# The pooling stage of a two-layer decoder trunk: scale by a broadcast transfer, whole-row loads of x, another order of the work, and the norms' epsilon on VectorE

## The chip, the core and the metric

The kernel runs on one core of a Trainium2 chip. A core has five engines that run side by side and wait for one another by semaphores: TensorE (PE, matmuls into the accumulators in PSUM), VectorE (DVE, elementwise work and statistics), ScalarE (ACT, casts and activations), GpSimd (POOL) and SyncE (SP, which issues transfers). Each engine takes its instructions strictly in the order of the program. The metric is device time in microseconds (us) of one execution; the kernel before takes 951.83 us, the median of three runs (950.6 to 952.05).

## The reference

The input is `x`, 512 tokens of 1024 float32. Layer 0 mixes tokens by pooling, layer 1 by attention; each is followed by a gated feed-forward, and each of the four steps ends in a layer norm. The part that matters here is layer 0's mixer and the norms:

```python
ALPHA = (2.0 * DEPTH) ** 0.25          # DEPTH = 2
POOL_WINDOWS = (2, 4, 8, 16)           # one group of 256 columns each

def _layernorm(x, g, b):
    mu = jnp.mean(x, axis=-1, keepdims=True)
    var = jnp.mean(jnp.square(x - mu), axis=-1, keepdims=True)
    return (x - mu) * lax.rsqrt(var + LN_EPS) * g + b

def _multiscale_pool(x, w, scale):
    ...                                # per group: mean over the last `win` tokens
    mixed = jnp.einsum('bsgc,gcd->bsgd', pooled - xg, w)
    return mixed.reshape(B, S, D) * scale

for i in range(DEPTH):
    h = pool(x) if i == 0 else diff_attention(x)
    x = _layernorm(ALPHA * x + h, ...)
    x = _layernorm(ALPHA * x + _swiglu(x, w_gate[i], w_up[i], w_down[i]), ...)
```

## The kernel before

**Numbers in two parts.** Float32 products are made from float32r operands: each operand is split into a high part (a cast on ACT) and a low part (the difference, on DVE or POOL), and `mm3` adds three products. So every block of data and of weights costs one cast, one subtraction and three matmuls for one.

**The order** is written out by hand: `tc.manual_schedule()` keeps each engine's instructions in the order of the Python code, and semaphores are put in for the data. The weights come in pieces of 128 x 1024 (512 KB), `raw0`, `raw1`, ..., through five buffers that SP fills in turn (`fetch`); `ready(c)` splits them up to number c.

**The pooling stage.** The 512 tokens are four blocks of 128 (s = 0 to 3). Pooling over tokens is a matmul with banded matrices, built on the core: `fh` (with its low part `fl`, which is not zero for the first 16 tokens only) for block 0, `bh` for the others. The helpers, in the order of their first use:

- `load_x(s)` loads block s of x into `res`; `split_x(s, d)` splits one half of its columns. In blocks 2 and 3 the low parts are made on POOL.
- `WARM` matmuls on zeros (`still`) stand first on PE.
- `spread(c)` makes 512 columns of the scale over all 128 partitions, by a matmul of one row of ones with one row of scale (`scrow`), into the accumulators `sc0` and `sc1`; `scale_weights(c)` multiplies the pool weights `raw0` and `raw1` by them on DVE, and `pool_weights(c)` splits them.
- `low(t, ks)` pools into tokens 0 to 255 from block t (t = 0, 1), `high(blocks, ks)` into tokens 256 to 511 from blocks 1 to 3. `split_pooled(half, groups)` brings the sums from PSUM to SBUF in two parts.
- `mixed(s, d)` multiplies block s by half d of the pool weights (12 matmuls of 256 columns), `summed(s, d)` adds it to `res` (`residual`) and takes the statistics (`stat`).
- `spread_of(n, s)` makes of them mean and variance (`mv`) and the factor `rs`: epsilon is added on POOL, and the power −0.5 taken on POOL. `norm(n, s)` applies them to `res` on DVE.
- `transposed(n, s)` turns a normed block on PE in eight matmuls into accumulators `pt`; `turned_half` applies gain and bias (ACT, one half of block 1 on DVE as `second`), `split_turned` splits into `xt`, the operand of the feed-forward.

`ready`, `tbh`, `tbl`, `ohr` and `lines_sum` in between split the first feed-forward weights and prepare the table of attention's biases.

**What follows.** `ffn(0)`, `attention`, `ffn(1)`. A feed-forward starts with three (layer 0) or two (layer 1) plain column blocks, tokens 0 to 255 first; blocks 2 and 3 of the layer are transposed between those products (`late`). Then come column blocks by Strassen products (`strassen(k)`, k from 2), with sums of weights (`weight_sums`, two DVE passes, then stores) and of hidden rows (`sum_hidden`) on DVE beside them. The last feed-forward ends with four norms in two passes each, which also add gain and bias (`norm` with `done`), and with the stores. Attention's end (`gather`) loads the table of activation functions for the next feed-forward (`preload_act_table_set`).

## Time and profile before

| | us |
|---|---|
| median of three runs | 951.83 (950.6 to 952.05) |
| the profiled execution | 952.55 |
| its span, first to last instruction | 950.8 |
| TensorE busy | 935.4 (98% of the span) |
| VectorE busy | 819.2 (86%) |
| ScalarE busy | 503.8 (53%) |
| POOL busy | 119.7 (13%) |
| HBM traffic | 206 GB/s over the span |

The profile is one execution, and every row below has its times in us from the start of the span. A timeline row has start, duration, engine, line, operation, what it writes and reads (the program's names, without buffer numbers) and, in brackets, how long the engine stood idle before it and what released it. PE is TensorE's matmuls. A busy PE is not PE at its peak: the rows also show how far apart the matmuls start.

### The profile page before, as it was taken

Reading aid. Unit: us, or ns where it says so; the run is one execution under the profiler, and the core shown is the slowest. Engines: PE = TensorE matmul, PEld = TensorE weight load, DVE = VectorE, ACT = ScalarE, POOL = GpSimd, SP = SyncE. Lnnn points to the kernel's source line nnn. Section 1 sums busy time; section 2 is a strip of 40 time slices with the busy share of each in tenths; the row PEclk is TensorE's granted clock in tenths of the full one; section 3 lists DMA queues with packets and bytes.
Section 4 is the critical chain, followed back from the end, with each engine's and each line's share of the span. In section 5 each row is a group of like instructions: output and inputs, shape, how many; then the busy total and the mean of one; then the engine's idle time right before and its main releaser. Section 6 shows DMA issues by size and latency. Waiting matters only on the chain.

```text
span 950.8 us, 16040 instructions
## 1 busy us (share of the span) xinstructions
PE 935.4 (98%) x6263; PEld 858.0 (90%) x6263; DVE 819.2 (86%) x1199; ACT 503.8 (53%) x807; POOL 119.7 (13%) x157
## 2 busy tenths in 40 slices
PE   9999999999999999999999999999999999999995
PEld 8899999999988888988888888999999999988884
DVE  6999999999988798688777676799999999987797
ACT  5563455555563467665566553834545544654450
POOL 5122111110001201000000000311111110002102
PEclk9999999999999999999999999999999999999998
DMA  7189998886877965423222122389988885878962
GB/s 255 44 250 270 298 293 264 261 241 221 260 241 261 361 206 166 145 89 100 77 80 80 65 90 89 115 254 283 285 248 257 263 274 203 250 237 287 321 212 88
DMA packets 73933, 196.88 MB, mean 207 GB/s; under 512 B 6595, under 2 KB 18019, under 8 KB 73858
## 3 DMA queue, kind: packets, MB, share of 16 engines
q1 hardware_dynamic: 34272, 113.92, 36.1%
q0 software_dynamic: 15952, 47.31, 18.8%
q10 hardware_dynamic: 23634, 34.64, 10.0%
q8 instruction: 49, 0.80, 0.3%
q14 instruction: 26, 0.21, 0.1%
HBM read 159.12 MB, written 36.72 MB: 206 GB/s over the span
## 4 chain that ended last, share of the span: by engine, by line
PE 85%; DVE 8%; ACT 3%; issue 2%; POOL 1%; POOLq 0%; DVEq 0%; ACTq 0%
PE A L851 21%; PE P L917 13%; PE C L851 10%; PE Q L917 6%; PE B L851 5%; PE s L1134 2%; PE v L125 2%; PE v L126 2%; PE v L127 2%; PE q L126 2%; PE q L127 1%; PE q L125 1%; PE k L125 1%; PE k L127 1%; PE k L126 1%
## 5 line engine op out<-in xcount | busy, mean ns | idle before, releaser
L605 DVE TENSOR_TENSOR raw<-raw,raw 128x1024 f32<-128x1024 f32 x72 | 87.8, 1219 | 0.6
L107 ACT CAST xs<-hid 128x512 fp32r<-128x512 f32 (+1 forms) x60 | 34.7, 581 | 28.4 <-DVE hid L770 28.4
L108 DVE TENSOR_TENSOR xs<-hid,xs 128x512 fp32r<-128x512 f32 (+1 forms) x60 | 38.4, 641 | 7.8 <-ACT xs L107 7.8
L227 ACT ACTIVATE y<-pt,gbT 128x128 f32<-128x128 f32 x92 | 34.6, 457 | 18.5 <-PE pt L208 18.4
L1144 ACT ACTIVATE p<-p,mn 128x128 f32<-128x128 f32 (+3 forms) x64 | 35.4, 554 | 14.9 <-DVE mn L1139 14.9
L701 POOL DMA_DIRECT2D b<-in_wall x24 | 18.1, 798 | 152.3 <-DMA tsum<-b 73.0
L762 POOL DMA_DIRECT2D xs<-ssum x24 | 17.4, 727 | 141.9 <-PE Q L917 119.3
L108 POOL TENSOR_TENSOR sql<-sq,sqh 128x512 fp32r<-128x512 f32 x7 | 9.1, 1295 | 165.3 <-ACT sqh L107 165.3
L877 ACT ACTIVATE sg<-sg 128x512 f32<-128x512 f32 x18 | 11.4, 633 | 33.2 <-DVE sg L870 33.2
L1139 DVE CUSTOM_DVE_ANT_0 p<-s,bias 128x128 f32<-128x128 f32 (+3 forms) x64 | 28.1, 485 | 0.0
L701 POOL DMA_DIRECT2D hid<-in_wall x20 | 14.8, 742 | 93.2 <-DVE g_42l L611 24.3
L171 POOL TENSOR_SCALAR rs<-mv 128x1 f32<-128x1 f32 x16 | 7.8, 490 | 147.2 <-DVE mv L169 143.2
L108 DVE TENSOR_TENSOR xt<-y,xt 128x512 fp32r<-128x512 f32 x23 | 15.6, 687 | 12.5 <-ACT xt L107 12.2
L738 ACT CAST v<-u 128x512 fp32r<-128x512 f32 x22 | 13.7, 621 | 22.6 <-DVE u L736 22.6
L862 ACT COPY hid<-C 128x512 f32<-128x512 f32 x18 | 10.6, 587 | 26.0 <-PE C L851 24.1
L163 DVE BATCH_NORM_STATS2 st<-res 128x6 f32<-128x512 f32 x32 | 22.2, 695 | 1.1
L108 DVE TENSOR_TENSOR heads<-k,heads 128x512 fp32r<-128x512 f32 x8 | 5.5, 692 | 20.2 <-ACT heads L107 20.2
L866 DVE TENSOR_TENSOR hid<-C,hid 128x512 f32<-128x512 f32 x18 | 12.4, 690 | 11.6 <-PE C L851 10.0
L702 POOL DMA_DIRECT2D b<-in_wall x12 | 14.7, 1229 | 56.8 <-DMA b<-in_wall 47.2
L1158 DVE SCALAR_TENSOR_TENSOR p<-p,sm,p 128x128 f32<-128x128 f32 (+3 forms) x32 | 17.6, 551 | 1.1
L107 ACT CAST heads<-k 128x512 fp32r<-128x512 f32 x8 | 4.7, 588 | 26.2 <-PE k L127 26.2
L1134 PE MATMUL s<-heads 64*128 64x256 f32 (+2 forms) x192 | 17.9, 330 | 0.0
(1154 smaller groups left out, 3822.2 us busy)
## 6 DMA issues: line engine op xcount, KB each, us to landing
raw<-in_wall SPq DMA_DIRECT2D x122, 512.0 KB, 4.4
r<-tsum SPq DMA_DIRECT2D x40, 512.0 KB, 4.4
b<-in_wall POOLq DMA_DIRECT2D x36, 512.0 KB, 6.0
hid<-in_wall POOLq DMA_DIRECT2D x30, 512.0 KB, 6.6
r<-in_wall SPq DMA_DIRECT2D x30, 512.0 KB, 4.5
tsum<-b ACTq DMA_DIRECT2D x24, 512.0 KB, 4.8
ssum<-v ACTq DMA_DIRECT2D x22, 512.0 KB, 3.7
tsum<-hid ACTq DMA_DIRECT2D x20, 512.0 KB, 5.1
```

The source lines that it names most:

```text
L107: nc.scalar.copy(dst_h, src)
L108: (low or nc.vector).tensor_tensor(dst_l, src, dst_h.bitcast(F32), op=ALU.subtract)
L125: nc.tensor.matmul(acc, ah, bh, start=start, stop=False)
L126: nc.tensor.matmul(acc, ah, bl, start=False, stop=False)
L127: nc.tensor.matmul(acc, al, bh, start=False, stop=stop)
L227: nc.scalar.activation(y[:, k, :], src, AF.Identity, bias=b, scale=g)
L605: tt(t, raws[pair[0]], raws[pair[1]], op=ALU.add)
L701: nc.gpsimd.dma_start(out=t[:, j], in_=src[:, j])
L851: nc.tensor.matmul(o, w[:, c], x[:, kk, :], start=p in ("P1", "Q5", "P2") and f + kk + e == 0, stop=p in ("Q4", "Q3", "P2") and (f, kk, e) ...
L917: nc.tensor.matmul(accs[s], x[:, k, r], y[:, c], start=first and k == 0 and e == 0, stop=last and k == m - 1 and e == 2, skip_group_check= ...
L1134: nc.tensor.matmul(accs[c][:, :wide], a[r, qs], b[r, :wide], start=i == 0, stop=i == 2)
L1144: nc.scalar.activation(p, p, AF.Exp, bias=mn[:, q, c : c + 1], scale=-1.0, accum_out=sm[:, q, c : c + 1],)
```

## The change

- The scale comes by one transfer on SP's queue, broadcast to 128 partitions (`scale`); the row, the ones, the two matmuls of `spread` and their accumulators go. `scale_weights` reads SBUF.
- x is loaded in four transfers of whole rows instead of eight of half rows.
- There are 22 warm-up matmuls instead of 5, and `fl` is 256 columns wide (zero beyond the 16, filled by ACT), so the low-part matmuls of block 0 are too.
- The accumulators for tokens 256 to 511 are taken from the start, and the order is another: block 1's high part follows the low parts at once, blocks 2 and 3 come later and one by one, their low parts and that of weight 2 are made on DVE, and `pool_weights` works in halves.
- The norms' epsilon is added on DVE, all 16 times.
- One pair of weight sums in each feed-forward stands behind the first Strassen product instead of a plain block. The line that loads the activation table stands behind its loop.

```diff
-WARM = 5
+WARM = 22
     def load_x(s):
-        for d in range(2):
-            c = slice(d * 512, (d + 1) * 512)
-            nc.sync.dma_start(out=res[:, s, c], in_=x[s * P : (s + 1) * P, c])
+        nc.sync.dma_start(out=res[:, s, :], in_=x[s * P : (s + 1) * P, :])
...
-        nc.gpsimd.tensor_scalar(rs, mv[:, 1:2], scalar1=EPS, scalar2=None, op0=ALU.add)
+        nc.vector.tensor_scalar(rs, mv[:, 1:2], scalar1=EPS, scalar2=None, op0=ALU.add)
         nc.gpsimd.tensor_tensor(rs, rs, mhalf, op=ALU.pow)
...
         load_x(0)
-        scrow = pp.tile([1, D], F32, name="scrow")
-        nc.scalar.dma_start(out=scrow, in_=pscale)
...
         load_x(1)
         fetch(1)
+        scale = pp.tile([P, D], F32, name="scale")
+        nc.sync.dma_start(out=scale, in_=pscale.broadcast_to([P, D]))
         load_x(2)
...
-        fl = pp.tile([P, 4, 16], F32R, name="fl")
+        fl = pp.tile([P, 4, 256], F32R, name="fl")
...
-        nc.vector.memset(fl.bitcast(F32), 0.0)
+        nc.scalar.copy(
+            fl.rearrange("p g (a t) -> p (g a) t", a=2), still.unsqueeze(1).to_broadcast([P, 8, P])
+        )
...
         for i in range(WARM):
-            nc.tensor.matmul(scb[0][:, 0:P], still, still, start=True, stop=True)
+            nc.tensor.matmul(warm[:, 0:P], still, still, start=True, stop=True)
...
-                    mm(o[:, :16], xk(xnh, 0, k), fl[:, g, :], start=False, stop=False)
+                    mm(o, xk(xnh, 0, k), fl[:, g, :], start=False, stop=False)
...
-        spread(0)
         low(0, range(4))
         low(0, range(4, 8))
-        spread(1)
         low(1, range(8))
-        for g in range(4):
-            made[1, g] = bank(f"pool1_{g}")
         scale_weights(0)
-        split_x(2, 0, nc.gpsimd)
-        split_x(2, 1, nc.gpsimd)
-        high((1, 2), range(4))
-        scale_weights(1)
+        high((1,), range(8))
         pool_weights(0)
-        split_x(3, 0, nc.gpsimd)
         split_pooled(0, 0, 1)
         mixed(0, 0)
+        split_x(2, 0)
+        split_x(2, 1)
+        high((2,), range(8))
+        scale_weights(1)
+        split_pooled(0, 2, 3)
         pool_weights(1)
-        split_pooled(0, 2, 3)
-        split_x(3, 1, nc.gpsimd)
-        high((1, 2), range(4, 8))
+        mixed(1, 0)
         mixed(0, 1)
-        ready(3, nc.gpsimd)
+        split_x(3, 0)
+        split_x(3, 1)
+        summed(0, 0)
...
-        mixed(1, 0, 1)
-        summed(0, 0, 1)
+        mixed(1, 1)
+        summed(0, 1)
         spread_of(0, 0)
+        ready(3)
...
-        summed(3, 0, 1)
+        summed(3, 0)
         norm(0, 2)
+        ready(5)
+        summed(3, 1)
         spread_of(0, 3)
-        ready(5)
         norm(0, 3)
...
-                if f in (3, 5, 7):
-                    weight_sums()
...
+                    if k == SPLIT[0] and p == "P1":
+                        weight_sums()
```

Three places show what this does to the queues. The first is the start of PE's. `still` is the zero operand, `sc0` the scale's accumulator, `pool0_0` the first group of tokens 0 to 255. Before:

```order
L314 MATMUL sc0_140<-still_100 128x128 x5
L345 MATMUL sc0_140<-scrow_81,one_101 128x512
L352 MATMUL pool0_0_136<-fh_97,xt_63 128x256
L353 MATMUL pool0_0_136<-fl_98,xt_63 128x16
L354 MATMUL pool0_0_136<-fh_97,xt_63 128x256
```

Now:

```order
L312 MATMUL pool1_0_134<-still_96 128x128 x22
L351 MATMUL pool0_0_130<-fh_93,xt_63 128x256
L352 MATMUL pool0_0_130<-fl_94,xt_63 128x256
L353 MATMUL pool0_0_130<-fh_93,xt_63 128x256
L351 MATMUL pool0_0_130<-fh_93,xt_63 128x256
```

Seventeen warm-ups came in, the one-row matmul went, and the 16-column matmul has 256 columns.

The second place is DVE's queue from the scaling of the pool weights on. `raw` are the weights, `pw` their low parts, `pooled` the low parts of the pooled sums, `xt<-res` those of x, `mix` the mixer's results. Before:

```order
L326 TENSOR_TENSOR raw0_87<-raw0_87,sc0_140 128x512 x2
L326 TENSOR_TENSOR raw1_91<-raw1_91,sc1_141 128x512 x2
L108 TENSOR_TENSOR pw0l_66<-raw0_87,pw0h_65 128x1024
L108 TENSOR_TENSOR pooled_64<-pool0_0_136,pooled_64 128x2x256
L108 TENSOR_TENSOR pooled_64<-pool0_1_137,pooled_64 128x2x256
L108 TENSOR_TENSOR pw1l_250<-raw1_91,pw1h_249 128x1024
L108 TENSOR_TENSOR pooled_64<-pool0_2_138,pooled_64 128x2x256
L108 TENSOR_TENSOR pooled_64<-pool0_3_139,pooled_64 128x2x256
L156 SCALAR_TENSOR_TENSOR res_67<-res_67,mix0_0_235 128x512
```

Now:

```order
L325 TENSOR_TENSOR raw0_83<-raw0_83,scale_85 128x512 x2
L337 TENSOR_TENSOR pw0l_66<-raw0_83,pw0h_65 128x512 x2
L106 TENSOR_TENSOR pooled_64<-pool0_0_130,pooled_64 128x2x256
L106 TENSOR_TENSOR pooled_64<-pool0_1_131,pooled_64 128x2x256
L106 TENSOR_TENSOR xt_63<-res_67,xt_63 128x512 x2
L325 TENSOR_TENSOR raw1_88<-raw1_88,scale_85 128x512 x2
L106 TENSOR_TENSOR pooled_64<-pool0_2_132,pooled_64 128x2x256
L106 TENSOR_TENSOR pooled_64<-pool0_3_133,pooled_64 128x2x256
L337 TENSOR_TENSOR pw1l_277<-raw1_88,pw1h_276 128x512 x2
L106 TENSOR_TENSOR xt_63<-res_67,xt_63 128x512 x2
L154 SCALAR_TENSOR_TENSOR res_67<-res_67,mix0_0_236 128x512
L161 BN_STATS st0_0_313<-res_67 128x6
```

Four passes over x (blocks 2 and 3) came in between, and the second weight's scaling moved behind the first pooled sums.

The third place is DVE's queue at the end of the stage, around the norms of blocks 2 and 3 (`mv0_2`, `mv0_3`). Before:

```order
L156 SCALAR_TENSOR_TENSOR res_67<-res_67,mix2_0_391 128x512
L163 BN_STATS st0_2_494<-res_67 128x6
L156 SCALAR_TENSOR_TENSOR res_67<-res_67,mix2_1_392 128x512
L163 BN_STATS st0_2_494<-res_67 128x6
L169 BN_AGGR mv0_2_498<-st0_2_494 128x2
L156 SCALAR_TENSOR_TENSOR res_67<-res_67,mix3_0_461 128x512
L163 BN_STATS st0_3_504<-res_67 128x6
L156 SCALAR_TENSOR_TENSOR res_67<-res_67,mix3_1_462 128x512
L163 BN_STATS st0_3_504<-res_67 128x6
L181 TENSOR_SCALAR res_67<-res_67,mv0_2_498,rs0_2_500 128x1024
L169 BN_AGGR mv0_3_509<-st0_3_504 128x2
L108 TENSOR_TENSOR w4l_517<-raw4_289,w4h_516 128x1024
```

Now:

```order
L161 BN_STATS st0_2_505<-res_67 128x6
L154 SCALAR_TENSOR_TENSOR res_67<-res_67,mix2_1_402 128x512
L161 BN_STATS st0_2_505<-res_67 128x6
L167 BN_AGGR mv0_2_509<-st0_2_505 128x2
L169 TENSOR_SCALAR rs0_2_511<-mv0_2_509 128x1
L154 SCALAR_TENSOR_TENSOR res_67<-res_67,mix3_0_472 128x512
L161 BN_STATS st0_3_515<-res_67 128x6
L179 TENSOR_SCALAR res_67<-res_67,mv0_2_509,rs0_2_511 128x1024
L106 TENSOR_TENSOR w4l_521<-raw4_317,w4h_520 128x1024
L154 SCALAR_TENSOR_TENSOR res_67<-res_67,mix3_1_473 128x512
L161 BN_STATS st0_3_515<-res_67 128x6
L167 BN_AGGR mv0_3_526<-st0_3_515 128x2
```

The norm of block 2 moved ahead of the second residual of block 3, weight 4's low part with it, and each aggregate is followed by the epsilon.

More of the change, by code (lines that the diff above doesn't have):

```diff
@@ L299, in trunk @@
         for t in (fh[:, :, 0:144], bh[:, :, P : P + 144]):
+            nc.vector.tensor_copy(t[:, :, P:], near[:, :, P:])
             nc.vector.tensor_tensor(t[:, :, :P], near[:, :, :P], own, op=ALU.subtract)
-            nc.vector.tensor_copy(t[:, :, P:], near[:, :, P:])
         xnh, xnl = (
@@ L309, in split_x @@
             split(xnh[:, s, c], xnl[:, s, c], res[:, s, c], low=low)
-        made = {(0, g): bank(f"pool0_{g}") for g in range(4)}
-        scb = [bank(f"sc{c}") for c in range(2)]
+        made = {(i, g): bank(f"pool{i}_{g}") for i in range(2) for g in range(4)}
+        warm = made[1, 0]
         for i in range(WARM):
-            nc.tensor.matmul(scb[0][:, 0:P], still, still, start=True, stop=True)
-        split(fh[:16, :, 0:16], fl[:16], d0)
+            nc.tensor.matmul(warm[:, 0:P], still, still, start=True, stop=True)
+        split(fh[:16, :, 0:16], fl[:16, :, 0:16], d0)
         split_x(0, 0)
@@ L325, in scale_weights, with pool_weights @@
                 r = raw[:, j * 512 : (j + 1) * 512].rearrange("p (k e) -> p k e", k=2)
-                nc.vector.tensor_tensor(
-                    r,
-                    r,
-                    scb[c][:, j * GW : (j + 1) * GW].unsqueeze(1).to_broadcast([P, 2, GW]),
-                    op=ALU.mult,
+                e0 = c * 512 + j * GW
+                engine.tensor_tensor(
+                    r, r, scale[:, e0 : e0 + GW].unsqueeze(1).to_broadcast([P, 2, GW]), op=ALU.mult
                 )
-        def pool_weights(c):
+        def pool_weights(c, between=lambda: None):
             h, l = weight_pair(f"pw{c}") if c else first_pair
-            split(h, l, raws.pop(c))
+            raw = raws.pop(c)
+            cols = [slice(j * 512, (j + 1) * 512) for j in range(2)]
+            for cc in cols:
+                nc.scalar.copy(h[:, cc], raw[:, cc])
+            between()
+            for cc in cols:
+                nc.vector.tensor_tensor(l[:, cc], raw[:, cc], h[:, cc].bitcast(F32), op=ALU.subtract)
             pw.append((h, l))
@@ L342, in xk @@
             return t[:, s, k * P : (k + 1) * P]
-        def spread(c):
-            mm(scb[c], one, scrow[:, c * 512 : (c + 1) * 512], start=True, stop=True)
         def low(t, ks):
@@ L451, in trunk @@
         norm(0, 0)
+        transposed(0, 0)
+        split_pooled(1, 0, 1)
         summed(1, 1)
         spread_of(0, 1)
-        transposed(0, 0)
-        split_pooled(1, 0, 1)
-        norm(0, 1)
         mixed(2, 0)
         split_pooled(1, 2, 3)
+        norm(0, 1)
+        mixed(2, 1)
         transposed(0, 1)
-        mixed(2, 1)
         pts = [turns.pop((0, i)) for i in range(2)]
```

7 lines of the change are left out of this document (2 added, 5 removed).

## The prediction

> **What bounds the kernel now.** I read the page first: its busy times, then the shares of the chain that ended last.
>
> ```profile
> span 950.8 us, 16040 instructions
> PE 935.4 (98%) x6263; PEld 858.0 (90%) x6263; DVE 819.2 (86%) x1199; ACT 503.8 (53%) x807; POOL 119.7 (13%) x157
> PE 85%; DVE 8%; ACT 3%; issue 2%; POOL 1%; POOLq 0%; DVEq 0%; ACTq 0%
> ```
>
> TensorE (PE) carries nearly everything, so a change outside it counts only where PE waits or where PE is slow. PE's timeline of the first 19 us shows slow work: columns are start, duration, instruction, and in brackets the idle time before it.
>
> ```profile
> 1.04 2.50 PE L314 MATMUL sc<-still 128*128 128x128 f32 x10 [1.04 <-DVE still L265]
> 3.48 2.07 PE L345 MATMUL sc<-scrow,one 1*128 1x512 f32 x2
> ...
> 10.12 0.41 PE L352 MATMUL pool<-fh,xt 128*128 128x256 f32 x1
> 10.34 0.21 PE L353 MATMUL pool<-fl,xt 128*128 128x16 f32 x1
> ...
> 10.90 2.07 PE L345 MATMUL sc<-scrow,one 1*128 1x512 f32 x2
> 12.90 0.58 PE L356 MATMUL pool<-bh,xt 128*128 128x256 f32 x1
> 13.28 0.41 PE L357 MATMUL pool<-bh,xt 128*128 128x256 f32 x1
> ...
> 17.97 0.40 PE L367 MATMUL pool<-bh,xt 128*128 128x256 f32 x1
> 18.18 0.31 PE L366 MATMUL pool<-bh,xt 128*128 128x256 f32 x1
> 18.33 0.28 PE L367 MATMUL pool<-bh,xt 128*128 128x256 f32 x1
> 18.45 0.28 PE L366 MATMUL pool<-bh,xt 128*128 128x256 f32 x1
> ```
>
> The 22 starts from 13.28 to 17.97 lie 0.213 us apart; from 18.33 on they lie 0.115 apart. The page's slices print a full clock there:
>
> ```profile
> PEclk9999999999999999999999999999999999999998
> ```
>
> But the spacing says that PE ran at about half rate until 18.2 and doubled there, 5.3 us after a dense run of 128-row, 256-column matmuls began at 12.90. Ahead of it stood one-row matmuls (L345) and 16-column ones (L353), and the rate did not rise behind them.
>
> After 19 us the stage depends more and more on VectorE (DVE). Three rows of its timeline, and PE's one large wait of the stage, at the transposes of block 2:
>
> ```profile
> 26.32 0.69 DVE L163 BATCH_NORM_STATS2 st<-res 128x6 f32<-128x512 f32 x1
> 26.93 0.80 DVE L181 TENSOR_SCALAR res<-res,mv,rs 128x1024 f32<-128x1024 f32 x1
> 27.65 0.68 DVE L156 SCALAR_TENSOR_TENSOR res<-res,mix 128x512 f32<-128x512 f32 x1
> ...
> 44.94 1.06 PE L208 MATMUL pt<-ident,res 128*128 128x128 f32 x8 [1.00 <-DVE mv L169]
> ```
>
> From 44.94 to 375 PE's timeline has no bracket, so the start of these transposes is the mark of the stage: what it gains, the kernel gains. After that brackets over 0.2 come at two norms only:
>
> ```profile
> 375.40 1.09 PE L208 MATMUL pt<-ident,res 128*128 128x128 f32 x8 [0.24 <-DVE res L181]
> 592.23 1.09 PE L208 MATMUL pt<-ident,res 128*128 128x128 f32 x8 [0.77 <-DVE res L181]
> ```
>
> Last, the tail. PE's last matmul starts at 938.60, yet the kernel ends at 950.8 behind four norms:
>
> ```profile
> 930.58 0.20 DVE L169 BATCH_NORM_AGGREGATE mv<-st 128x2 f32<-128x12 f32 x1
> 930.81 1.42 DVE L188 SCALAR_TENSOR_TENSOR res<-res,mv,gb 128x512 f32<-128x512 f32 x2
> 930.87 0.78 POOL L171 TENSOR_SCALAR rs<-mv 128x1 f32<-128x1 f32 x1 [18.71 <-DVE mv L169]
> 931.74 0.92 POOL L172 TENSOR_TENSOR rs<-rs,mhalf 128x1 f32<-128x1 f32 x1
> 932.70 1.41 DVE L192 SCALAR_TENSOR_TENSOR res<-res,rs,gb 128x512 f32<-128x512 f32 x2 [0.47 <-POOL rs L172]
> ...
> 942.37 0.68 DVE L904 SCALAR_TENSOR_TENSOR res<-res,P 128x512 f32<-128x512 f32 x1
> ...
> 938.60 0.39 PE L917 MATMUL P<-d_41h,xs 128*128 128x512 f32 x1
> ```
>
> **The change, part by part.**
>
> *Warm-up and first matmuls.* Ten halves of five warm-ups took at most 3.48 − 1.04 = 2.44 us, so 0.244 each at half rate, 0.12 at full. Now there are 44. If they count as dense work, the rate doubles 5.3 us after 1.04, at 6.3; 22 are done by then, 22 more take 2.6: PE is free at 9.0. If they do not count, at 1.04 + 44 × 0.244 = 11.8. The one-row matmuls go (2 × 2.0 us), and the low parts of block 0 become 256 wide: 24 + 4 matmuls at 0.115 = 3.2 us bring the first pooled group to 12.2. In before ScalarE (ACT) had it at 14.16, and block 1 of x was there at 7.33, so the blocks are no obstacle:
>
> ```profile
> 7.33 0.62 ACT L107 CAST xt<-res 128x512 fp32r<-128x512 f32 x1 [1.14 <-DMA res<-in_x]
> 14.16 0.59 ACT L107 CAST pooled<-pool 128x512 fp32r<-128x512 f32 x1 [0.75 <-PE pool L357]
> ```
>
> The whole widening of L353 costs PE 8 × 0.1 us at full rate, and that lies ahead of S + 1.9 below, where nobody waits for PE.
>
> The Trainium skill, "TensorE: Matmul & The Clock Gate", Part 1, says that the first 3.4 us or so of matmuls run at half clock, by time and not by count, and that a window without work longer than that drops it again. Taken as a rule of time alone it would have put before at full rate by 7.9; the trace disagrees, with 0.213 us spacing until 18.2. By its window the rise in the changed kernel would come between 4.5 and 7.9, which gives 8.1 to 9.8 for the 9.0 above.
>
> *Scale by a transfer.* The scaling of the first pool weights waits for the broadcast, fourth on SP's queue: 2 MB with what stands ahead of it. In before the second half of block 2 was the end of the same 2 MB:
>
> ```profile
> 10.43 0.62 ACT L107 CAST xt<-res 128x512 fp32r<-128x512 f32 x1 [0.36 <-DMA res<-in_x]
> 12.79 0.62 ACT L107 CAST xt<-res 128x512 fp32r<-128x512 f32 x1 [0.80 <-DMA res<-in_x]
> ...
> gb<-in_lng SPq DMA_DIRECT2D x1, 512.0 KB, 4.2
> gb<-in_lnb SPq DMA_DIRECT2D x1, 512.0 KB, 6.6
> ```
>
> So S, its landing, is 10.4. Of the two broadcast loads of gb, issued together, the second took 2.4 us longer than the first; here 512 KB of weights and 256 KB of block 3 came between 10.43 and 12.79, which is 1.6 us for 512 KB. A broadcast at 2.4 instead of 1.6, and a little more, gives the late end 11.5. The early end is 9.5: x's whole rows need half the issues, and a transfer's length less is the most that they can win. What SP queues behind it comes one such length later each: block 2 at 12.0, weight 1 at 13.6, block 3 at 15.2. DVE wants them at S + 3.8 = 14.2, 15.4 and 19.1, so moving them back is hidden; with that cover gone (a broadcast over 2 us late) each us would be paid.
>
> *DVE's queue.* It takes over from POOL the low parts of blocks 2 and 3 and of weight 2; two memsets go, and POOL is left with the powers alone. Prices:
>
> ```profile
> 5.04 1.90 DVE L108 TENSOR_TENSOR xt<-res,xt 128x512 fp32r<-128x512 f32 x3 [0.31 <-ACT xt L107]
> 51.95 1.22 DVE L611 TENSOR_TENSOR g_5l<-raw,g_5h 128x1024 fp32r<-128x1024 f32 x1
> 53.08 2.35 DVE L650 TENSOR_TENSOR hid<-xt 128x1024 f32<-128x1024 f32 x2
> 385.00 0.14 DVE L1036 TENSOR_SCALAR gcol<-gcol 128x1 f32<-128x1 f32 x1
> ```
>
> Three 512-column passes in 1.90 are 0.61 apart; a 1024-column pass 1.13 (51.95 to 53.08); a residual with its statistics 1.32 (two passes and a hand-over); a norm 0.72 (26.93 to 27.65); aggregate plus epsilon 0.36 (0.23 as from 930.58 to 930.81, and 0.13 for the one-column pass). From S: 16 passes of 512 (9.8) and a wait of 0.2 for ScalarE; two residuals 2.64, 0.36, weight 2 and tbl 1.2, a residual 1.32, norm of block 0 0.75: it ends at S + 16.3 = 26.7. Then four pooled passes 2.44, a residual 1.32, 0.36, norm of block 1 0.75: S + 21.2 = 31.6. Then low parts, weight 3 and `second` 4.9; block 2's two residuals 2.64, 0.36, block 3's first residual 1.32, norm of block 2 0.75: S + 31.2 = 41.6.
>
> PE beside it: transposes of block 1 after 31.6 (0.9), mixes of block 3 24 × 0.12 = 2.9, lines 0.7, 48 first matmuls of the feed-forward at 0.12 = 5.8: 41.9. So block 2's transposes start at about 42.0 against 44.94: 2.9. I take off 0.2 for hand-overs that the sum lacks: **2.7 us**. The order helps here: block 2's norm no longer stands behind the second residual of block 3 (1.32).
>
> PE gets ahead of DVE in the middle: from 9.0 its 136 matmuls up to block 3's high part end at 25.3, and block 0's transposes wait for the norm at 26.7. This wait, 1.4 us, or 2.3 with PE free at 8.1, is in the sum: it is the next thing late.
>
> *Epsilon on DVE.* In the tail the norm's first pass starts 0.23 after the aggregate and the second 1.89 later. Now: 0.23, then 0.13 more, then 1.33 for two passes back to back; the power on POOL, 0.92, starts 0.46 after the aggregate and is done 1.38 after it, before 1.69. So 2.12 becomes 1.69, four times: **1.7 us**. PE does not step in: block 3's residual at 942.37 moves by three norms' gains, 1.3, and stays behind the matmul at 938.60, which shifts with all else. Bounds: 4 × (0.47 − 0.14) = 1.3, and 4 × 0.47 = 1.9. At 375.40 and 592.23 PE waits for the same chain:
>
> ```profile
> 590.45 0.22 POOL L171 TENSOR_SCALAR rs<-mv 128x1 f32<-128x1 f32 x1 [35.40 <-DVE mv L169]
> ```
>
> The add leaves it with its hand-over (0.22 + 0.09) and one pass of 0.13 enters: 0.2 each, **0.4**. Elsewhere after the stage no bracket of PE hangs on a norm.
>
> *Weight sums one step later, the act table line lower.* The two sums (1.3 us of DVE) of one step move from ahead of `sum_hidden`'s differences to behind them. PE's next hand-over from DVE in the second feed-forward is this row, and it stands behind them in both orders:
>
> ```profile
> 668.57 0.68 DVE L868 TENSOR_TENSOR hid<-hid,A 128x512 f32<-128x512 f32 x1
> ```
>
> So they are paid on DVE as before and give 0; at best the operands that now pass them come 1.3 us sooner, at worst their store, and the next load behind it, go out that much later, and no PE bracket hangs on those. The table load keeps its place in ScalarE's order: 0.
>
> *Sum.* 2.7 + 1.7 + 0.4 = 4.8. The sum is made against the profiled execution, 952.55 (span 950.8), which is 0.72 above the median 951.83. From the median: **947.0**. Below 0.2%, 1.9 us, a measurement here cannot tell a change from none.
>
> **The rivals.**
>
> 1. *The clock does not heed the warm-ups* (their operands are zero, and no row shows warm-ups alone raising it). PE starts at 11.8 at half rate; the first pooled group comes at 11.8 + 28 × 0.213 = 17.8 if the rate rises at 18 as in before. ACT wants it at S + 1.9, so the chain acts as with S = 15.9: block 2 at 47.5 and 0.2 of hand-overs, 2.8 late, less 2.1 for the rest: 952.5. With the rise 5.3 after 11.8 some 0.4 better. For it: the zeros. Against: the one-row and 16-column matmuls explain the slow start alone. Chance 0.13.
> 2. *The clock falls in PE's new wait ahead of block 0's transposes.* Half rate until 5.3 us of dense work have passed does 2.7 us less work on the path after 31.6, and block 0's transposes take 0.9 more: 3.6, so 950.6. Against: the wait is 1.4 to 2.3 us, and behind the wait of 1.0 at 44.94 the rate stayed. By the window of 3.4 us in the Trainium skill, "TensorE: Matmul & The Clock Gate", Part 1, it would stay as well; no run here shows a wait of that length. Chance 0.08.
> 3. *The other side: the broadcast lands late*, because 128 partitions read one row. DVE's chain behind S is rigid, so each us of S costs one: the stage breaks even at S = 13.1, the kernel at 15.2, and from 17.1 it is slower by over 0.2%. At S = 18 it takes 954.6. For it: nothing moves until S, neither DVE nor ACT, and no other step of the change can be late by that much. Against: the gb rows, 4.2 and 6.6. Chance 0.07.
>
> **How the numbers follow.** The forecast has 0.72; the rivals 0.13, 0.08 and 0.07. The likeliest case reaches from 945.2 (S 9.5, tail 1.9, the runs' scatter of 0.7) to 949.2 (S 11.5, tail 1.3, scatter). The range of 8 in 10 goes to 944.8 below, for a sum of hand-overs that is smaller than taken, and to 950.8 above, which takes in rival 2. Faster by over 0.2% are the forecast and a third of rival 2: 0.75; within 0.2% rival 1 and the rest of 2: 0.18; slower rival 3: 0.07.
>
> **What would show it.** PE's spacing near 0.115 before 10 us; L325 on DVE starting at 10 to 11; DVE without a bracket over 0.5 from there to 40; block 2's transposes at 42; no 0.47 bracket ahead of the tail's second passes; the two waits at norms 0.2 shorter. Wrong would be: spacing of 0.21 beyond 10 us, L325 after 12, or PE slow again after its wait at 24.

## The result: 945.98 us, 5.8 faster, and the profile after

The changed kernel takes 945.98 us (median of four runs, 945.69 to 948.01) against 951.82 for the kernel before; the ratio is 0.9946, 95% interval 0.9929 to 0.9963, so 3.5 to 6.8 us faster. The profiled execution took 946.19, 0.21 above the median. Forecast was 947.0 with a range of 944.8 to 950.8.

The page's first lines of the changed kernel: TensorE is busy for 99% of a span 6.4 us shorter.

```profile
span 944.4 us, 16089 instructions
PE 932.3 (99%) x6293; PEld 858.9 (91%) x6293; DVE 823.5 (87%) x1220; ACT 505.8 (54%) x810; POOL 104.9 (11%) x136
```

PE's timeline of the changed kernel in the stage: the warm-ups, block 0's first matmul, and the transposes of blocks 0, 2 and 3.

```profile
1.06 7.77 PE L312 MATMUL pool<-still 128*128 128x128 f32 x44 [1.06 <-DVE still L262]
8.58 0.36 PE L351 MATMUL pool<-fh,xt 128*128 128x256 f32 x1
26.84 1.81 PE L206 MATMUL pt<-ident,res 128*128 128x128 f32 x8 [1.82 <-DVE res L179]
42.55 1.03 PE L206 MATMUL pt<-ident,res 128*128 128x128 f32 x8
46.30 1.04 PE L206 MATMUL pt<-ident,res 128*128 128x128 f32 x8
```

PE leaves the warm-ups at 8.58 and waits 1.82 ahead of block 0's transposes. These take 1.81 instead of about 1.05: the clock has fallen. A table by stretch (PE busy and instructions, then the other engines, granted clock, DMA) shows half rate from 27.0 to 30.4:

```profile
core 0: us, PE busy (x) PEld busy (x) DVE busy (x) ACT busy (x) POOL busy (x), PEclk, DMA share, GB/s
27.00:30.40 3.40, 3.40 (x18) 3.40 (x18) 3.30 (x8) 2.71 (x8) 0.56 (x1) 0.50 0.12 47
```

Block 2's transposes start at 42.55 against 44.94 before, 2.39 earlier. The better mark is block 3's, 46.30 here and in before:

```profile
48.79 1.03 PE L208 MATMUL pt<-ident,res 128*128 128x128 f32 x8
```

That is 2.49 earlier. In before PE waited for DVE's norm at block 2 (the bracket of 1.00 at 44.94) and came to block 3's transposes by its own work, without a bracket. The new order takes block 2's norm forward; with it the place where DVE holds PE up moves to block 3's norm, as the runs below show. Behind this mark PE needs 889.61 us to its last matmul in the changed kernel (46.30 to 935.91) and 889.81 in before (48.79 to 938.60), so all that lies between gained 0.20, at the two norms (brackets of 0.24 and 0.77 before):

```profile
372.83 1.09 PE L206 MATMUL pt<-ident,res 128*128 128x128 f32 x8 [0.20 <-DVE res L179]
589.53 1.09 PE L206 MATMUL pt<-ident,res 128*128 128x128 f32 x8 [0.62 <-DVE res L179]
```

DVE in the stage of the changed kernel: the scaling waits for the broadcast, the first pooled low part for PE and ScalarE; the norms of blocks 0, 1, 2 and 3 are the L179 rows.

```profile
8.98 1.29 DVE L325 TENSOR_TENSOR raw<-raw,scale 128x512 f32<-128x512 f32 x2 [1.29 <-DMA scale<-in_pscale]
12.78 1.29 DVE L106 TENSOR_TENSOR pooled<-pool,pooled 128x512 fp32r<-128x512 f32 x2 [1.12 <-ACT pooled L105]
25.90 0.80 DVE L179 TENSOR_SCALAR res<-res,mv,rs 128x1024 f32<-128x1024 f32 x1
30.78 0.80 DVE L179 TENSOR_SCALAR res<-res,mv,rs 128x1024 f32<-128x1024 f32 x1
40.88 0.80 DVE L179 TENSOR_SCALAR res<-res,mv,rs 128x1024 f32<-128x1024 f32 x1
45.30 0.81 DVE L179 TENSOR_SCALAR res<-res,mv,rs 128x1024 f32<-128x1024 f32 x1 [0.73 <-POOL rs L170]
```

And the tail. The 0.47 ahead of the second passes is gone:

```profile
926.61 0.20 DVE L167 BATCH_NORM_AGGREGATE mv<-st 128x2 f32<-128x12 f32 x1
926.84 0.15 DVE L169 TENSOR_SCALAR rs<-mv 128x1 f32<-128x1 f32 x1
926.91 1.40 DVE L186 SCALAR_TENSOR_TENSOR res<-res,mv,gb 128x512 f32<-128x512 f32 x2
927.15 0.93 POOL L170 TENSOR_TENSOR rs<-rs,mhalf 128x1 f32<-128x1 f32 x1 [19.46 <-DVE rs L169]
928.24 1.41 DVE L190 SCALAR_TENSOR_TENSOR res<-res,rs,gb 128x512 f32<-128x512 f32 x2
935.91 0.39 PE L915 MATMUL P<-d_41h,xs 128*128 128x512 f32 x1
940.00 1.41 DVE L190 SCALAR_TENSOR_TENSOR res<-res,rs,gb 128x512 f32<-128x512 f32 x2
```

From the aggregate to the second pass it takes 1.63 (926.61 to 928.24) instead of 2.12, four times 0.49. One more distance differs, and is called the lead from here on: DVE's first aggregate of the tail starts 9.30 ahead of PE's last matmul instead of 8.03. The end differs too, from DVE's last pass to the end of the span: 950.76 less 947.35 before, 944.41 less 941.41 now. So the two traces differ by 2.49 (stage) + 0.20 (two norms) + 1.27 (lead) + 1.96 (tail) + 0.4 (end) = 6.3, and the span is 6.35 shorter. The 1.27 and the 0.4 were in no forecast.

### The profile page after: what moved, and what is told of

Read it like the earlier page. It is cut to its first block, busy times and chain, and to the rows that moved or that the text cites. A ratio compares the mean times of both kernels' runs of the same rounds, so it can differ in the third digit from the quotient of the medians.

```text
span 944.4 us, 16089 instructions
## 1 busy us (share of the span) xinstructions
PE 932.3 (99%) x6293; PEld 858.9 (91%) x6293; DVE 823.5 (87%) x1220; ACT 505.8 (54%) x810; POOL 104.9 (11%) x136
## 5 line engine op out<-in xcount | busy, mean ns | idle before, releaser
L170 POOL TENSOR_TENSOR rs<-rs,mhalf 128x1 f32<-128x1 f32 x16 | 12.6, 791 | 167.8 <-DVE rs L169 167.8
```

## The experiments

Theory: in the new order DVE's queue is rigid from the first pooled low part to block 3's norm (12.78 to 46.11 = 33.3 us here, 33.0 to 33.3 in the five traces with all on DVE and wide low parts), so the stage is worth what that start gains; the start is set by the later of the scale's landing and PE's first pooled group, and PE's by the clock. The tail is worth 4 x 0.49. The rivals stand in the expectations. Times in the text are medians; comparisons are with before, run beside each (951.8 to 952.0 beside the first eight kernels, 951.5 beside the next three), or with the changed kernel (945.98).

**Epsilon alone**, on the kernel before:

```diff
-        nc.gpsimd.tensor_scalar(rs, mv[:, 1:2], scalar1=EPS, scalar2=None, op0=ALU.add)
+        nc.vector.tensor_scalar(rs, mv[:, 1:2], scalar1=EPS, scalar2=None, op0=ALU.add)
```

> The kernel before with one line changed: the norms' epsilon on DVE. Theory (the prediction's): the four norms of the tail lose a hand-over each. The changed kernel's trace has 1.63 us from an aggregate to the second pass (926.61 to 928.24) where before had 2.12, so 4 x 0.49 = 2.0, and 0.1 to 0.2 at each of the two norms that PE waits for: 2.1 to 2.4 us faster than before, about 949.6, PE's last matmul 0.2 to 0.4 earlier. Rival 1: epsilon also explains why DVE's first aggregate of the tail stood 3.97 us earlier while PE stood only 2.69 earlier: then 3.4 to 3.7 faster, 948.3. Rival 2: the stores behind the norms hold the end: under 1 us.

949.70, ratio 0.9979 (0.9971 to 0.9988): 2.1 faster by the medians, 1.1 to 2.8 by the interval. Its start of block 3's transposes, and its tail:

```profile
49.47 1.03 PE L208 MATMUL pt<-ident,res 128*128 128x128 f32 x8
929.71 0.20 DVE L169 BATCH_NORM_AGGREGATE mv<-st 128x2 f32<-128x12 f32 x1
931.34 1.41 DVE L192 SCALAR_TENSOR_TENSOR res<-res,rs,gb 128x512 f32<-128x512 f32 x2
939.01 0.39 PE L917 MATMUL P<-d_41h,xs 128*128 128x512 f32 x1
```

1.63 from aggregate to second pass again. This trace also has the lead of 9.30 (929.71 to 939.01), but a gain of 3.4, as by rival 1, lies outside the interval, so the lead is not what epsilon brings.

**Five warm-ups** in the changed kernel:

```diff
-WARM = 22
+WARM = 5
```

> The changed kernel with 5 warm-ups instead of 22. Theory A: any dense window of 128-row matmuls raises the clock, and the wide low parts are enough. PE then starts block 0 at about 5.4 instead of 8.58, runs at 0.213 us a matmul and doubles at 9 to 12.3; the first pooled group (28 matmuls) is done at 11.4 at the latest, against 11.95 with 22 warm-ups. Time: from 0.6 us faster to equal to the changed kernel. Theory B: the warm-ups are what the early clock needs. Then the rate stays at 0.213 until about 18 as in before, mix(0,1), for which DVE waited 0.19 at 21.59, comes some 2 us later and so does DVE's chain: about 2 us slower than the changed kernel, 948.

945.05 (944.64 to 946.7), ratio 0.9934 (0.9921 to 0.9946): not slower than with 22, so theory A. PE's rows:

```profile
5.12 0.55 PE L351 MATMUL pool<-fh,xt 128*128 128x256 f32 x1 [1.56 <-ACT xt L105]
25.34 1.63 PE L206 MATMUL pt<-ident,res 128*128 128x128 f32 x8 [2.22 <-DVE res L179]
44.77 1.06 PE L206 MATMUL pt<-ident,res 128*128 128x128 f32 x8
```

Block 0 starts 3.46 earlier, the rate doubles at 8.61 in the midst of its matmuls, and DVE's first pooled low part starts at 11.57 instead of 12.78, now bound by the scale (8.98 + 2.59). Block 3's transposes come 1.53 earlier, although the clock fell here too, from 25.67 to 29.09, behind the wait of 2.22. Warm-ups on zeros raise the clock, and so does the real work once it is dense; 17 of the 22 only stood ahead of it.

**The wait filled**: eight matmuls on zeros ahead of block 0's transposes, in their own accumulator.

```diff
+        for i in range(fill):
+            nc.tensor.matmul(turns[n, s][0][:, 0:P], still, still, start=True, stop=True)
...
-        transposed(0, 0)
+        transposed(0, 0, still, 8)
```

> The changed kernel with eight matmuls on zeros ahead of block 0's transposes, in the 1.82 us in which PE waits for the norm. In the changed kernel's trace the clock fell for 3.41 us behind this wait (27.0 to 30.4) and block 2's transposes started at 42.55 without a bracket, 0.87 after DVE had their operand (41.68). Theory: the fall costs PE 1.7 us of work and 0.85 us on the path; with PE kept busy the clock stays, block 2's transposes start at 41.7 to 41.8 and the kernel gains up to 0.85 against a run with the fall, 0 against one without: 945.1 to 946.0. Rival: the clock falls all the same, since eight matmuls on zeros do not fill the window: transposes at 42.55 or later, no gain.

946.68 (946.23 to 949.19), ratio 0.9953 (0.9940 to 0.9967): no gain. The clock stayed at full rate to the end, and yet:

```profile
26.70 1.04 PE L208 MATMUL pt<-ident,res 128*128 128x128 f32 x8
41.98 1.03 PE L208 MATMUL pt<-ident,res 128*128 128x128 f32 x8
46.12 1.06 PE L208 MATMUL pt<-ident,res 128*128 128x128 f32 x8 [0.23 <-DVE res L179]
```

Block 2's transposes gained 0.57 and block 3's 0.18, then PE waits 0.23 for DVE's norm of block 3. The fall costs PE 1.7 us of work (half of 3.41) in a stage that DVE's queue bounds. This run showed that the new order's mark is block 3, not block 2.

**Weight sums back** behind the plain block:

```diff
                 gated(order[f], *a)
+                if f in (3, 5, 7):
+                    weight_sums()
...
-                    if k == SPLIT[0] and p == "P1":
-                        weight_sums()
```

> The changed kernel with the one pair of weight sums of each feed-forward back behind the plain block. The prediction has 0 for this part: the same time within 0.5 us, PE's last matmul the same. Rival: this move is what let the loads of the last weight sums (d_24 and on) land 5.6 us earlier, and so DVE's first aggregate of the tail stand 1.28 us further ahead of PE: then 1.0 to 1.3 us slower than the changed kernel, all of it behind PE's 900th us.

947.01 (945.32 to 947.79), ratio 0.9948 (0.9935 to 0.9960). The medians differ by 1.0, and the two intervals overlap. The trace has the same 889.60 from block 3's transposes to PE's last matmul, and the lead of 9.30:

```profile
45.27 1.06 PE L206 MATMUL pt<-ident,res 128*128 128x128 f32 x8 [0.24 <-DVE res L179]
925.57 0.20 DVE L167 BATCH_NORM_AGGREGATE mv<-st 128x2 f32<-128x12 f32 x1
934.87 0.39 PE L915 MATMUL P<-d_41h,xs 128*128 128x512 f32 x1
```

So in this execution the moved sums give 0 on PE's path, and the long lead stands without the move. But the trace is of the fastest of five runs, and 1.0 is what the rival asks for: whether the sums' old place makes a short lead more frequent is not shown. Up to block 3 this program is the changed kernel itself, and yet it stands 1.03 earlier there: its clock rose at 4.94, that of the changed kernel at 6.51. That much comes from when the clock rises in an execution.

**The clock alone**, on the kernel before: 22 warm-ups and 256-column low parts, which ScalarE clears as in the changed kernel (the lines for that are left out here); all else as it was.

```diff
-WARM = 5
+WARM = 22
...
-        fl = pp.tile([P, 4, 16], F32R, name="fl")
+        fl = pp.tile([P, 4, 256], F32R, name="fl")
```

> The kernel before with the 22 warm-ups and the 256-column low parts alone; scale still by one-row matmuls, old order, epsilon on POOL. Theory: an early clock helps before only where DVE waits for mixes that PE makes late (1.37 at 20.75 and 1.84 at 24.00, 3.2 together). PE reaches full rate at 5 to 8 instead of 18.2, leaves the warm-ups at 7.8 to 8.8 instead of 3.5, and is some 1.8 us further by 18.2, so block 3's transposes start about 1.8 earlier than 48.8: 950.0. Rival 1: the order and the transfer of the scale carry the whole gain of the stage, and the clock alone gives 0: 951.8. Rival 2: the clock carries it all (2.5): 949.3.

949.93, ratio 0.9980 (0.9971 to 0.9988): 2.0 faster by the medians, 1.1 to 2.8 by the interval. That fits the theory's 1.8; rival 1 (nothing) is out, rival 2 (2.5) is not. The rate doubled at 6.68, and block 3's transposes start 1.4 and 0.5 earlier than in the two traces of before (48.79 and 47.93); this execution, 951.26, is the slowest of its twelve:

```profile
47.41 1.04 PE L208 MATMUL pt<-ident,res 128*128 128x128 f32 x8
```

**The scale late**: its transfer issued behind block 3 of x.

```diff
         fetch(1)
-        scale = pp.tile([P, D], F32, name="scale")
-        nc.sync.dma_start(out=scale, in_=pscale.broadcast_to([P, D]))
         load_x(2)
         fetch(2)
         load_x(3)
+        scale = pp.tile([P, D], F32, name="scale")
+        nc.sync.dma_start(out=scale, in_=pscale.broadcast_to([P, D]))
```

> The changed kernel with the scale's broadcast issued behind block 3 of x, three transfers later: S moves from 8.98 to about 12.9 to 13.4 (three transfers at 1.3 to 1.5 us). Theory: in the changed kernel DVE's chain starts with the first pooled low part at 12.78, which waited for PE; by S alone it would be 8.98 + 2.6 = 11.6, so the first 1.2 us of delay are free and each us behind that costs one: chain at 15.5 to 16.0, 2.7 to 3.2 slower than the changed kernel, 948.7 to 949.2. Rival (the prediction's sum, S + 16.3 from the landing on): all 3.9 to 4.4 are paid, 949.9 to 950.4. Rival 2: PE's slack hides it: under 1.

949.67 (948.83 to 951.95), 3.7 slower than the changed kernel by the medians; ratio to before 0.9978 (0.9969 to 0.9987) against the changed kernel's 0.9946, which makes 3.0 us.

```profile
13.21 1.30 DVE L325 TENSOR_TENSOR raw<-raw,scale 128x512 f32<-128x512 f32 x2 [5.46 <-DMA scale<-in_pscale]
15.81 1.28 DVE L106 TENSOR_TENSOR pooled<-pool,pooled 128x512 fp32r<-128x512 f32 x2
48.99 1.06 PE L206 MATMUL pt<-ident,res 128*128 128x128 f32 x8 [0.24 <-DVE res L179]
```

S moved by 4.23, the pooled low part by 3.03, block 3's transposes by 2.69 against the changed kernel's trace: the first 1.2 us are free, as PE was later than the scale there. The rest, 1.0 by the medians and 0.4 by the ratios, is not explained by the stage; this execution (950.89, above its median) also has a lead of 7.59 only.

**Low parts on POOL.** Since DVE's queue bounds the stage, work was taken off it, with 5 warm-ups: first the low parts of block 3 and of weight 2, then those of weights 3 and 4 as well.

```diff
-        split_x(3, 0)
-        split_x(3, 1)
+        split_x(3, 0, nc.gpsimd)
+        split_x(3, 1, nc.gpsimd)
...
-        ready(3)
+        ready(3, nc.gpsimd)
```

The second of the two also has these:

```diff
-        nc.vector.tensor_tensor(l, raws.pop(3), h.bitcast(F32), op=ALU.subtract)
+        nc.gpsimd.tensor_tensor(l, raws.pop(3), h.bitcast(F32), op=ALU.subtract)
...
+        ready(5, nc.gpsimd)
         summed(2, 0, 1)
...
         norm(0, 2)
-        ready(5)
         summed(3, 1)
```

> The changed kernel with 5 warm-ups, and the low parts of block 3 of x and of weight 2 back on POOL. Theory: behind the first pooled low part DVE's queue is rigid (33.2 us to the norm of block 3 in three traces); without 1.2 us for block 3 and 1.14 for weight 2 it takes 30.9, and block 3's transposes start at 42.4 instead of 44.8 with 5 warm-ups: 2.3 faster than those, 942.7. Rival 1: PE is the next bound: it then reaches block 0's transposes at 23 and needs 17.8 us of work to block 3's, 40.8, so no. Rival 2: DVE's passes slow down while POOL works beside them (one took 1.64 instead of 1.22 in before), or POOL's slow passes (1.25 to 1.3 for 512 columns, 2.43 for 1024) come late for PE: half of the gain, 943.9, or none.

> As the kernel with 5 warm-ups and two low parts on POOL, and the low parts of weights 3 and 4 on POOL too. Theory: DVE's queue loses another 2 x 1.14 us; PE's own work (23 + 17.8 = 40.8 for block 3's transposes) is then reached: 1.6 to 2.3 faster than with two, about 940.8. Rival: weight 3 or 4 comes late from POOL (2.43 each) and PE waits for it in the first feed-forward: no gain, or a loss of 1.

946.03 (945.85 to 946.31), ratio 0.9938 (0.9926 to 0.9950), and 947.04 (946.26 to 947.73), 0.9946 (0.9933 to 0.9959). The medians are 1.0 and 2.0 above the 945.05 with all on DVE; the intervals overlap, so a loss is not shown, but the forecast gains are not there. DVE's queue from the first pooled low part to block 3's norm took 33.53 and 33.23 us, against 33.05 with all on DVE: the work that was taken off it did not shorten it. DVE and POOL of the first of the two:

```profile
17.00 2.39 DVE L337 TENSOR_TENSOR pw1l<-raw,pw1h 128x512 fp32r<-128x512 f32 x2
24.05 2.24 DVE L179 TENSOR_SCALAR res<-res,mv,rs 128x1024 f32<-128x1024 f32 x1
17.14 3.40 POOL L106 TENSOR_TENSOR xt<-res,xt 128x512 fp32r<-128x512 f32 x2 [10.87 <-ACT xt L105]
23.35 2.38 POOL L106 TENSOR_TENSOR w2l<-raw,w2h 128x1024 fp32r<-128x1024 f32 x1
```

Two DVE passes that take 1.28 together took 2.39, and a norm of 0.80 took 2.24, while POOL worked: 2.5 us lost, about as much as DVE was spared (1.2 and 1.14). DVE's passes that read PSUM and its statistics (0.67 to 0.69) were not held up. The Trainium skill, "SBUF — State Buffer", section "Who interferes with whom", says that DVE and GpSimd share a pair of ports under an exclusive lock: a DVE instruction with two inputs in SBUF contends with a GpSimd instruction that reads SBUF, one in a two-port mode with any, and one with at most one SBUF input outside these modes with none. The rows of the low parts (2.39) and the residuals (0.67 to 0.69) agree with it; that the norm runs in a two-port mode no run here shows.

**Timed low parts.** Two runs, with 5 warm-ups as well, put POOL's work beside DVE passes of the kind that was not held up: weights 2 and 4, then block 3 too (ScalarE casting weight 3 first).

```diff
         spread_of(0, 0)
-        ready(3)
...
         split_pooled(1, 0, 1)
+        ready(3, nc.gpsimd)
         summed(1, 1)
...
+        ready(5, nc.gpsimd)
         summed(2, 0, 1)
...
         norm(0, 2)
-        ready(5)
         summed(3, 1)
```

The second of the two also has these:

```diff
-        split_x(3, 0)
-        split_x(3, 1)
...
         nc.scalar.copy(last_pair[0], raws[3])
+        split_x(3, 0, nc.gpsimd)
+        split_x(3, 1, nc.gpsimd)
```

> The changed kernel with 5 warm-ups, and the low parts of weights 2 and 4 on POOL at places where DVE only has passes that read PSUM, statistics and one-column passes. Theory: in the two kernels with low parts on POOL the DVE passes over SBUF alone were held up (norm of block 0 2.23 us instead of 0.80, low part of pool weight 1 2.39 for two instead of 1.29), those that read PSUM and the statistics were not (0.67 to 0.69). So placed, the two save 1.14 each: block 3's transposes at about 42.5 instead of 44.8, 2.2 faster than with 5 warm-ups, 942.9. Rival: POOL holds up whatever DVE does: no gain, 945 or more.

> As the one before, and block 3's low parts of x on POOL as well, beside DVE's residuals of block 0 (ScalarE casts weight 3 first, so that POOL starts as DVE's low part of pool weight 1 ends). Theory: another 1.2 us off DVE's queue; block 3's transposes at 41.3 to 41.5, the kernel 1.0 to 1.2 faster than the one before, about 941.8. Rival: POOL's two passes (2.5 us or more) come after PE wants them (about 20), PE waits and mix and norm stay where they were: no gain on the one before; or the low part of pool weight 1 is held up by 1.1 and the gain is gone.

944.16 (943.79 to 945.12), ratio 0.9922 (0.9909 to 0.9936), and 945.79 (943.85 to 946.24), 0.9933 (0.9921 to 0.9946). The first of the two:

```profile
23.46 0.80 DVE L179 TENSOR_SCALAR res<-res,mv,rs 128x1024 f32<-128x1024 f32 x1
27.46 1.29 DVE L106 TENSOR_TENSOR pooled<-pool,pooled 128x512 fp32r<-128x512 f32 x2
25.98 2.40 POOL L106 TENSOR_TENSOR w2l<-raw,w2h 128x1024 fp32r<-128x1024 f32 x1 [3.19 <-ACT w2h L105]
44.03 1.03 PE L206 MATMUL pt<-ident,res 128*128 128x128 f32 x8
```

None of these DVE passes is stretched. DVE's last norm of the stage ends at 43.15 instead of 44.62 (5 warm-ups), but block 3's transposes start at 44.03, 0.74 earlier and not the 2.3 of the forecast: PE, coming from block 2's, is the bound now. This is the fastest kernel of the study, 0.9 below the one with 5 warm-ups and 1.8 below the changed kernel by the medians, though its interval overlaps with both. The third low part adds nothing: DVE then waits for PE's mix, and its trace, of the fastest of five runs, stands 0.28 earlier.

```profile
20.01 0.69 DVE L154 SCALAR_TENSOR_TENSOR res<-res,mix 128x512 f32<-128x512 f32 x1 [0.94 <-PE mix L125]
```

**Narrow low part**: 5 warm-ups, and `fl` 16 columns wide and cleared on DVE as in before (the clearing's lines are left out here).

```diff
-        fl = pp.tile([P, 4, 256], F32R, name="fl")
+        fl = pp.tile([P, 4, 16], F32R, name="fl")
...
-                    mm(o, xk(xnh, 0, k), fl[:, g, :], start=False, stop=False)
+                    mm(o[:, :16], xk(xnh, 0, k), fl[:, g, :], start=False, stop=False)
```

> The changed kernel with 5 warm-ups and the low part of block 0 16 columns wide again (cleared on DVE as in before). Theory: 16-column matmuls leave PE's window too thin, so the clock waits for a whole window of block 1's matmuls (from 9.4) and rises between 12.9 and 16.2 instead of at 8.6; PE loses 1.7 to 3.4 us, mix(0,1) is done at 20.9 to 22.6 where DVE want it at 20.1, and the kernel is 0.8 to 2.5 slower than with 5 warm-ups and wide low parts: 945.9 to 947.6. Rival: time alone raises the clock, as the rule of the prediction's quoted page has it: then it rises at 8.6 or before, and the time is 945.0.

947.52 (945.86 to 948.41), ratio 0.9954 (0.9941 to 0.9968): 2.5 slower than with wide ones by the medians, though the intervals touch. The clock rose at 14.62 instead of 8.61, DVE waited 1.17 for a mix of PE, and block 3's transposes came 2.46 later:

```profile
47.23 1.06 PE L206 MATMUL pt<-ident,res 128*128 128x128 f32 x8
```

**Before, a second trace**, the kernel unchanged.

> The kernel before, unchanged, for a second trace of it. Open is why DVE's first aggregate of the tail stood 8.03 us ahead of PE's last matmul in the first trace of before and 9.30 ahead in the changed kernel's. Theory: the loads of the last weight sums land late in some executions of any kernel (in the first trace weight d_24 was cast 51.2 us ahead of PE's last matmul, in the changed kernel's 54.1); then this trace may show any lead from 7.6 to 9.3, together with the cast, and the rest as in the first: 889.8 us from block 3's transposes to PE's last matmul, 16.0 from the first aggregate to DVE's last pass, 4.17 behind it. Rival: before always has the short lead, 8.0, because of something that the change moved.

951.07, in a single run. The lead is 8.76 (929.09 to 937.85) in place of 8.03, so the same program gives two leads. As for weight d_24, which the theory names, its cast stands 51.18 ahead of PE's last matmul in before, 52.02 in this trace and 54.07 in the changed kernel's.

Over all fourteen traces the lead is 9.30 in seven and 7.6 to 8.8 in seven; both groups hold kernels with the old and with the new order. The cast of d_24 does not quite tell them apart: the first run with two low parts on POOL has it at 52.28 and still the lead of 9.30. The cast of d_27, three weights on, does: it stands 45.10 to 46.38 ahead where the lead is 9.30, and 43.15 to 44.34 where it is shorter. Here it is in before and in the changed kernel, then DVE's first residual of the tail in the same two, then this trace's block 3, first aggregate and last matmul:

```profile
895.00 1.05 ACT L107 CAST d_27h<-r 128x1024 fp32r<-128x1024 f32 x1 [1.45 <-DMA r<-tsum]
890.54 1.05 ACT L105 CAST d_27h<-r 128x1024 fp32r<-128x1024 f32 x1 [1.76 <-DMA r<-tsum]
924.67 0.68 DVE L904 SCALAR_TENSOR_TENSOR res<-res,P 128x512 f32<-128x512 f32 x1
920.69 0.69 DVE L902 SCALAR_TENSOR_TENSOR res<-res,P 128x512 f32<-128x512 f32 x1 [0.42 <-PE P L915]
47.93 1.03 PE L208 MATMUL pt<-ident,res 128*128 128x128 f32 x8
929.09 0.20 DVE L169 BATCH_NORM_AGGREGATE mv<-st 128x2 f32<-128x12 f32 x1
937.85 0.39 PE L917 MATMUL P<-d_41h,xs 128*128 128x512 f32 x1
```

In each of the seven traces with 9.30 that residual waits for PE (0.14 to 0.49); in the other seven it does not. So 9.30 is the lead of a DVE that has caught up with PE, and a shorter lead is that of one still behind when the tail comes. That the lateness varies from execution to execution is shown for before; what makes these loads late is not settled.

## Why the prediction was right, step by step

The time came out 1.0 below the forecast, inside the range, and the mechanism was in the main the forecast's. The forecast gain of 4.8 lies inside the measured interval (3.5 to 6.8), so the 1.0 is not clear of noise. Of the signs that the prediction named, three did not come as written: L325 started at 8.98 and not at 10 to 11, DVE had a bracket of 1.12 at 12.78, and PE was slow again behind its wait, which was to be a sign of being wrong. By its terms:

- *PE free of the warm-ups at 9.0, first pooled group at 12.2*: 8.58, and ScalarE had the group at 12.16. Right, with some luck: the clock rose at 6.51 where 6.3 was taken, but over five traces with 22 warm-ups it rose anywhere from 4.94 to 7.27. Rival 1 (zeros not heeded) fell.
- *S, the landing of the scale, at 10.4, 9.5 at the earliest*: wrong. The broadcast landed at 8.98, half a microsecond below the early end. I had priced it by the landings of half-row loads, and a broadcast at the price of the slower of two.
- *DVE's chain, norms at 26.7, 31.6, 41.6*: they ended at 26.70, 31.58 and 41.68, but partly by two errors that cancel: S was 1.4 early, and the wait of 1.12 for the first pooled group, which the sum did not have, and 0.19 for a mix gave it back. The rule "each us of S costs one" holds from 1.2 us of delay on only (the scale late).
- *PE waits 1.4 to 2.3 ahead of block 0's transposes*: 1.82.
- *Stage 2.7*: 2.39 at block 2's transposes and 2.49 at block 3's in this pair of traces. Block 3's transposes started at 48.79, 47.93 and, with epsilon alone, 49.47 in the old stage, and at 46.30, 46.12 and 45.27 in the new: 2.83 apart on the average. I took block 2's transposes for the mark, which they were in before; the filled wait showed that in the new order block 3's are. Block 2's came 0.87 behind their norm (41.68), and that cost 0.2 at block 3's.
- *Rival 2, the clock falls in PE's wait* (0.08, 950.6): its mechanism came true, in the profiled execution and in three more of the ten traces with the new order; its price did not. The argument against it, that a wait well under 3.4 us leaves the rate alone, was wrong. It cost 3.6 in my working, since I let half rate last 5.3 us and had nothing to cover it; it lasted 3.41, and block 3's norm on DVE covered all but some 0.2.
- *Rival 3, the broadcast late*: did not occur. Made to occur by 4.2 us it cost 2.7 in the stage.
- *Tail 1.7*: under-sized; 4 x 0.49 = 1.96, since the added pass delays the next by 0.07, not by the 0.13 that I took from a one-column pass elsewhere. *Two norms 0.4*: over-sized; 0.20. Together 2.16 for 2.1, two errors that cancel; epsilon alone measured 2.14 (1.1 to 2.8).
- *Weight sums 0*: in the one trace of it, their return left PE's path as it was; the medians cannot tell. The act table's line was not run by itself.
- *Not in the sum*: the 0.4 at the end, and the 1.27 of a shorter lead, from loads that came late in before's profiled execution. That execution was 0.72 above its median, so part of the 6.4 between the profiles is no gain of the change.

The parts, by runs: epsilon 2.1, the clock 2.0, each give or take 0.8; what is left of the 5.8, 1.7, is order, transfer, whole-row loads and the end together. These were not taken apart, and the parts need not add.

## What to carry to other kernels

Find the engine whose queue runs without a gap to the place where the next engine waits for it, and ask what starts that queue and what is in it: a late transfer, an early clock or a fall of the clock counts as far as it moves that queue, and no further. Make the first real matmuls dense before adding warm-ups: here 5 and wide operands did as well as 22, and narrow ones cost 2.5 us. Before moving work to POOL, look at what DVE does at that moment: beside passes that read PSUM DVE lost nothing here, beside passes over SBUF alone it lost what it had been spared.

## What the runs showed of the chip

*The clock rose at the end of the first 3.41 us window that was dense throughout, in all fourteen traces.* Dense means 128-row matmuls of 128 columns or more, with no gap. In the changed kernel's records the clock changes at 6.51, 26.99 and 30.41, which is 6 and 1 times 3.413 us apart; the windows are counted from these marks. With dense work from 12.90 (before) it rose at 16.41, 18.22 and 18.62; from 1.06 (22 warm-ups, five traces) at 4.94 to 7.27; from 5.1 to 5.2 (5 warm-ups, wide, five traces) at 8.61 to 11.16; from 10.78 (narrow) at 14.62: always 3.5 to 6.2 us behind the start of dense work, which is one whole window and a part of another. The prediction's rule quoted from the Trainium skill, "TensorE: Matmul & The Clock Gate", Part 1, gives the window and its free run rightly; that everything behind the first 3.4 us runs at the full rate, whatever the matmuls, these runs contradict, since 16-column matmuls between the wide ones kept it down (14.62 against 8.61). One-row matmuls stood ahead of every late rise of before; no run takes them out by themselves. The table in the same section of the Trainium skill has the clock fall after an idle window. Here less was enough: a wait of 1.82, 1.82, 2.12 or 2.22 us inside one window brought it down for one window, while 1.62 or less in a window did not, and in one trace 1.82 did not either.

*The phase of this window scatters the time.* Programs that are the same up to there differ by 1.03 us at block 3's transposes (45.27 and 46.30, with the rise at 4.94 and 6.51), before by 0.86 (47.93 and 48.79, with the rise at 16.41 and 18.22).

*The end of the kernel*, from DVE's last pass on, took 3.4 us in the four traces with before's transfers and 3.0 in the ten with the changed kernel's. SP's closing waits go through the transfers' semaphores one after the other, 0.06 us each. Behind the last store's, before had five more to go through, the changed kernel one: from that store's landing to SP's next step it took 0.39 and 0.14. That is 0.25 of the 0.4; the rest lies ahead of it and behind it. No run isolates it.
